# Two MLPs of a transformer kernel: the first product by pairs of output tiles with seven block products

## The chip, the cores and the metric

The kernel runs on one core of a Trainium2 chip. The metric is the time of the whole program on the device, in microseconds, as the median of three runs.

## The reference

The program computes two blocks of a transformer for 512 tokens of 1024 features, in float32. The change touches the squared-relu MLP, which the second block holds twice (`l` = 0 and 1), with 4096 hidden features:

```python
def squared_relu_mlp(h, w1, w2):
    return jnp.square(jax.nn.relu(h @ w1)) @ w2
...
        x = x + squared_relu_mlp(rms_norm_2(x, norm_mlp[layer]), mlp_w1[layer], mlp_w2[layer])
```

`h @ w1` is the first product, `... @ w2` the second. The attention and the mixers before, between and around the MLPs stay as they are.

## The kernel before

Activations stand feature-major: a tile holds 128 features as partitions and 512 tokens as columns. A float32 product is made of parts: each operand is split into a high part (a cast to float32r on ScalarE, `whi`, `xgh`, `hidh`) and a low part (the rest, a subtraction on VectorE, `wlo`, `xgl`, `hidl`), and `mm` (L287) multiplies high by high, high by low and low by high, three matmuls for each 128 rows of the contraction (L294 to L296). Each matmul is written with its own weight load.

`unit` (L254) loads one unit of weights, 128 x 1024 (the weights of one output tile for 8 tiles of the contraction, 512 KB), through SP's queue into a `raw` tile (L261), casts it (L269) and subtracts (L270). The pool `wp` holds two `raw`, two `whi` and two `wlo` tiles, used in turn. A tile is taken again when its last reader is done.

`mlp` (L901) goes through four chunks of 8 hidden tiles. In a chunk it makes the 8 hidden tiles one after the other (the first products: 8 x 3 matmuls of 512 columns into a PSUM bank of the ring `mm`, then relu out of PSUM (L917), square (L918) and the split into `hid` (L275, L276)), then 8 output tiles (the second products, from `hid`), each of which is scaled by R and added to x by VectorE (L909, L910). In the last chunk the last output tiles (4 in layer 0, 5 in layer 1) are made by halves of 256 tokens, so that what follows can begin with the first half.

PSUM has eight banks, cut into rings for a phase by `psum_phase`: in the MLPs six for `mm`, two for `t`.

The instructions are written in program order; a scheduler orders them for each engine when the program is built, by program order and by when it expects them to be ready, and sets the semaphores. On the chip each engine's order is then fixed. SP's queue issues the loads in order too, and a load whose buffer is not free holds those behind it.

## Time and profile before

| | us |
|---|---|
| median of three runs | 1986.74 |
| the three runs | 1985.92, 1986.74, 1994.5 |
| span of the profiled execution | 1986.7 |
| TensorE busy (share of the span) | 1906.8 (96%) |
| VectorE busy | 1169.8 (59%) |
| ScalarE busy | 885.8 (45%) |
| GpSimd busy | 400.8 (20%) |

The profiled execution's own time is its span; nothing lies around it. The profile tells for each engine when it was busy, with what, and what ended each idle time. PE stands for TensorE, PEld for its weight loads, DVE for VectorE, ACT for ScalarE, POOL for GpSimd, SP for the engine that issues the loads. A row of a matmul is longer than the distance to the next matmul's start, since matmuls overlap; the distance of the starts is the time that each takes of TensorE. PEclk is the granted clock of TensorE, as a share of its 2.4 GHz.

### The profile page before, as it was taken

The numbers are of one execution on the slowest core, as the hardware profiler recorded it, in microseconds if no ns is written. First come the engines' busy times: TensorE is split into PE (matmuls) and PEld (weight loads), VectorE is DVE, ScalarE is ACT, GpSimd is POOL, SyncE is SP. The second block draws the span as 40 slices with busy tenths as digits, with TensorE's granted clock in tenths as the row PEclk, the third lists the DMA queues.
The fourth block names the chain that finished last, engine by engine and source line by source line (L and its number), as shares of the span: only waits on it lengthen the run. The fifth ranks groups of instructions, "written<-read, shape, count | busy, mean of one in ns | idle before, by whom it ended". The sixth has DMA issues, their size and how long they took to land. (4 is left out here: it accounts for less than half of the span.)

```text
span 1986.7 us, 24617 instructions
## 1 busy us (share of the span) xinstructions
PE 1906.8 (96%) x9238; PEld 1566.1 (79%) x9238; DVE 1169.8 (59%) x1912; ACT 885.8 (45%) x1549; POOL 400.8 (20%) x374
## 2 busy tenths in 40 slices
PE   8688999999999999999999999989999999999997
PEld 6466788888888878888888888878878778888887
DVE  7979675335344874463434345869887963343435
ACT  6566654333233542234242434546666753324243
POOL 2777240000001420020000001235454430000001
PEclk9898999999999999999999999999999999999998
DMA  4121222222223222222223223254232122222222
GB/s 146 51 75 35 80 81 85 95 96 96 95 93 99 75 82 93 95 98 96 96 85 105 89 95 115 84 163 117 67 93 75 35 88 96 96 95 95 88 94 85
DMA packets 64551, 179.89 MB, mean 91 GB/s; under 512 B 7856, under 2 KB 16240, under 8 KB 64432
## 3 DMA queue, kind: packets, MB, share of 16 engines
q1 hardware_dynamic: 63600, 177.53, 28.0%
q8 instruction: 72, 1.18, 0.2%
q10 hardware_dynamic: 832, 0.79, 0.1%
q14 instruction: 47, 0.39, 0.1%
HBM read 165.71 MB, written 2.10 MB: 84 GB/s over the span
## 5 line engine op out<-in xcount | busy, mean ns | idle before, releaser
L269 ACT CAST whi<-raw 128x1024 fp32r<-128x1024 f32 (+4 forms) x324 | 303.6, 940 | 764.2 <-PE mm L295 680.6
L270 DVE TENSOR_TENSOR wlo<-raw,whi 128x1024 fp32r<-128x1024 f32 (+4 forms) x298 | 352.7, 1186 | 281.9 <-ACT whi L269 278.9
L294 PE MATMUL mm<-hidh,whi 128*128 128x512 f32 (+1 forms) x738 | 281.7, 382 | 1.0 <-DVE tmp L909 1.0
L296 PE MATMUL mm<-hidh,wlo 128*128 128x512 f32 (+1 forms) x738 | 281.4, 381 | 0.0
L295 PE MATMUL mm<-hidl,whi 128*128 128x512 f32 (+1 forms) x738 | 281.3, 381 | 0.0
L295 PE MATMUL mm<-xgl,whi 128*128 128x512 f32 (+1 forms) x608 | 233.6, 385 | 4.5 <-DVE xgl L279 3.2
L327 POOL TENSOR_TENSOR ssq<-ssq,sq 128x512 f32<-128x512 f32 (+1 forms) x61 | 71.8, 1177 | 810.2 <-ACT sq L324 809.1
L296 PE MATMUL mm<-xgh,wlo 128*128 128x512 f32 (+1 forms) x608 | 233.2, 384 | 0.4 <-DVE wlo L270 0.4
L294 PE MATMUL mm<-xgh,whi 128*128 128x512 f32 (+1 forms) x608 | 232.3, 385 | 0.6 <-ACT whi L269 0.6
L294 PEld LDWEIGHTS mm<-hidh,whi 128*128 128x128 f32 x738 | 138.4, 188 | 31.0 <-DVE tmp L909 1.2
L296 PEld LDWEIGHTS mm<-hidh,wlo 128*128 128x128 f32 x738 | 138.4, 188 | 29.8
L295 PEld LDWEIGHTS mm<-hidl,whi 128*128 128x128 f32 x738 | 138.4, 188 | 29.8
L295 PEld LDWEIGHTS mm<-xgl,whi 128*128 128x128 f32 x608 | 115.0, 189 | 31.0 <-DVE xgl L279 4.4
L909 DVE TENSOR_TENSOR tmp<-mm,R 128x512 f32<-128x512 f32 (+1 forms) x73 | 45.4, 624 | 155.6 <-PE mm L296 155.6
L294 PEld LDWEIGHTS mm<-xgh,whi 128*128 128x128 f32 x608 | 114.6, 189 | 25.8 <-ACT whi L269 1.5
L296 PEld LDWEIGHTS mm<-xgh,wlo 128*128 128x128 f32 x608 | 115.1, 189 | 24.7 <-DVE wlo L270 0.8
L411 ACT ACTIVATE pw<-pw,nm 128x512 f32<-128x512 f32 (+3 forms) x160 | 89.4, 560 | 55.5 <-DVE nm L409 54.5
L509 POOL TENSOR_TENSOR cy<-cy,tap 128x512 f32<-128x512 f32 x60 | 92.3, 1540 | 33.6 <-ACT tap L508 30.3
L276 DVE TENSOR_TENSOR hidl<-tmp,hidh 128x512 fp32r<-128x512 f32 x94 | 64.7, 689 | 37.0 <-ACT hidh L275 36.8
L511 DVE SCALAR_TENSOR_TENSOR cy<-cp,cols,cy 128x512 f32<-128x512 f32 x60 | 72.3, 1205 | 1.9 <-ACT cy L522 1.4
L409 DVE CUSTOM_DVE_ANT_0 pw<-s,tb 128x512 f32<-128x512 f32 (+3 forms) x128 | 59.0, 479 | 6.1 <-PE s L403 5.3
L276 DVE TENSOR_TENSOR ptl<-t,pth 128x384 fp32r<-128x384 f32 (+1 forms) x96 | 55.6, 591 | 9.1 <-ACT pth L275 9.0
(658 smaller groups left out, 4101.3 us busy)
## 6 DMA issues: line engine op xcount, KB each, us to landing
raw<-mlp SPq DMA_DIRECT2D x128, 512.0 KB, 3.4
raw<-a_in SPq DMA_DIRECT2D x24, 512.0 KB, 3.4
raw<-w_gate SPq DMA_DIRECT2D x22, 512.0 KB, 3.4
raw<-w_up SPq DMA_DIRECT2D x22, 512.0 KB, 3.4
raw<-w_down SPq DMA_DIRECT2D x16, 512.0 KB, 3.5
raw<-w_in SPq DMA_DIRECT2D x12, 512.0 KB, 3.6
raw<-a_out SPq DMA_DIRECT2D x8, 512.0 KB, 3.4
raw<-w_q SPq DMA_DIRECT2D x8, 512.0 KB, 3.8
```

Of the source, the lines that this page charges most:

```text
L269: S.copy(hi[:, a], raw[:, a])
L270: eng.tensor_tensor(lo[:, a], raw[:, a], hi[:, a], op=OP.subtract)
L276: (eng or V).tensor_tensor(l, src, h, op=OP.subtract)
L294: P.matmul(acc, hi[:, s], h, start=first and k == 0, stop=False)
L295: P.matmul(acc, hi[:, s], l, start=False, stop=False)
L296: P.matmul(acc, lo[:, s], h, start=False, stop=last and k == n - 1)
L327: (V if k >= self.n - 2 or self.fast else G).tensor_tensor(a, a, s[:, ts], op=OP.add)
L409: V.tensor_tensor_reduce(out=t, in0=s[:, :n], in1=tab[:, 384 - 128 * i:], op0=OP.add, op1=OP.min, scale=1.0, scalar=3.0e38, accum_out=nm[: ...
L411: S.activation(t, t, AF.Exp, bias=nm[:, i:i + 1], scale=-1.0, accum_out=rs[:, i:i + 1])
L509: G.tensor_tensor(conv_y[c], conv_y[c], t, op=OP.add)
L511: V.scalar_tensor_tensor(conv_y[c], cp[c][:, k:k + T], w, conv_y[c], op0=OP.mult, op1=OP.add)
L909: V.tensor_tensor(t, acc[:, ts], R[:, ts], op=OP.mult)
```

## The change

Two neighbouring output tiles of the first product, 2 x 2 blocks of weights (four contraction tiles each) and 2 x 2 blocks of inputs (the halves of the tokens, and the even and the odd contraction tiles) are multiplied with seven block products of sums in place of eight block products, in Winograd's form of Strassen's scheme. A block product is 4 x 3 matmuls of 256 columns. This is done for all pairs of a layer but the first, which stays two whole products: 15 pairs in each layer.

- The sums of the inputs (`pair_sums`) are made once per layer and kept split, four for each two contraction tiles.
- The sums of the weights are made in `pair_units`: of seven blocks of 128 x 512, which lie in a new order in DRAM (`_blocks`, 1792 KB for a pair), a tile `a` is loaded, a tile `s` is loaded and then another one added onto it by a DMA that GpSimd's queue issues, a half tile `z` is loaded, and a tile `u` is summed up on VectorE. Each of the four is split as before. Their `raw`, `whi` and `wlo` tiles come from `wp` and from a second pool of the same size, `sw`, in turn: a and u from `wp`, s and z from `sw`.
- `fast_pair` makes the products. The sums of products stay in PSUM where the scheme lets them: `y1` takes four of the products, `y4` two, `y2` one; three copies out of PSUM on ScalarE and three additions on VectorE make the two hidden tiles. The seventh product of a pair is written behind the fifth of the next (`late`).
- PSUM is cut into two banks `y1`, four `mm` and two `t`. In layer 1's last chunk four tiles instead of five go by halves. The weights of the halved tiles and the tiles of the output come from the two pools.

```diff
+def _blocks(w):
+    w = np.asarray(w)
+    m = w.shape[1]
+    a = w.reshape(4, 2, 128, m // 256, 2, 128).transpose(3, 4, 1, 2, 0, 5).reshape(m // 256, 2, 2, 128, 512)
+    b = [a[:, i, j] for i, j in ((0, 0), (0, 1), (1, 1), (0, 0), (1, 0), (1, 0), (1, 1))]
+    return np.ascontiguousarray(np.concatenate(b, 2))
...
-        A[f"mlp1_{l}"] = _units(I["mlp_w1_2"][l])
+        A[f"mlp1_{l}"] = _units(I["mlp_w1_2"][l])[:2]
+        A[f"mlp1f_{l}"] = _blocks(I["mlp_w1_2"][l])
...
+    B11, B12, B21, B22, T1, T3, T2, T4 = range(8)
+    def pair_sums(k, gain, pl, tpl):
+        b = pl.tile([128, 1024], FT, name="raw", bufs=2).rearrange("p (a t) -> p a t", a=4)
+        s = pl.tile([128, 1024], FT, name="raw", bufs=2).rearrange("p (a t) -> p a t", a=4)
+        for i in range(2):
+            S.activation(b[:, 2 * i:2 * i + 2], x[k + i].rearrange("p (a t) -> p a t", a=2), AF.Copy,
+                         scale=col(gain, k + i))
+        V.tensor_tensor(s[:, 0], b[:, B11], b[:, B12], op=OP.subtract)
+        V.tensor_tensor(s[:, 1], b[:, B22], b[:, B12], op=OP.subtract)
+        V.scalar_tensor_tensor(s[:, 2], s[:, 0], -1.0, b[:, B22], op0=OP.mult, op1=OP.subtract)
+        V.scalar_tensor_tensor(s[:, 3], s[:, 2], -1.0, b[:, B21], op0=OP.mult, op1=OP.subtract)
+        return split(s, *(tpl.tile([128, 4, T // 2], FR, name=f"xt{k}{p}") for p in "hl"))
+    def slots(tiles, sums):
+        return [[p[:, ts] for p in t] for t in tiles for ts in HALVES] + [[p[:, i] for p in sums] for i in range(4)]
+    def pair_units(src, rings):
+        def hl(r, n=1024):
+            pl = rings.pop(0)
+            rings.append(pl)
+            h, l = (pl.tile([128, 1024], FR, name=w, bufs=2)[:, :n] for w in ("whi", "wlo"))
+            return split(r[:, :n], h, l)
+        def raw():
+            pl = rings[0]
+            rings.append(rings.pop(0))
+            return pl.tile([128, 1024], FT, name="raw", bufs=2)
+        a, s, u, z = [raw() for _ in range(4)]
+        nc.sync.dma_start(a, src[:, :1024])
+        nc.sync.dma_start(s, src[:, 1024:2048])
+        nc.gpsimd.dma_start(s, src[:, 2048:3072], accum_op=OP.add)
+        nc.sync.dma_start(z[:, :512], src[:, 3072:])
+        ua = hl(a)
+        us = hl(s)
+        V.tensor_tensor(u[:, :512], s[:, 512:], z[:, :512], op=OP.add)
+        V.tensor_tensor(u[:, 512:], u[:, :512], a[:, 512:], op=OP.add)
+        return ua, us, hl(u), hl(z, 512)
+    late = []
+    def fast_pair(us, xps, pl, f, done):
+        ua, us_, uu, uz = us
+        H = T // 2
+        y1 = bank("y1")[:, :H]
+        y4 = bank("mm")[:, :H]
+        y2 = bank("mm")[:, :H]
+        def prod(acc, u, c0, slot, first):
+            hi, lo = u
+            for j, xp in enumerate(xps):
+                h, l = xp[slot]
+                s = slice(c0 + 128 * j, c0 + 128 * j + 128)
+                P.matmul(acc, hi[:, s], h, start=first and j == 0, stop=False, skip_group_check=True)
+                P.matmul(acc, hi[:, s], l, start=False, stop=False, skip_group_check=True)
+                P.matmul(acc, lo[:, s], h, start=False, stop=j == 3, skip_group_check=True)
+        def copy(acc):
+            t = pl.tile([128, H], FT, name="yc", bufs=4)
+            S.copy(t, acc)
+            return t
+        prod(y1, ua, 0, B11, True)
+        p1 = copy(y1)
+        prod(y4, us_, 0, T1, True)
+        p5 = copy(y4)
+        prod(y2, ua, 512, B21, True)
+        t1 = tmp()
+        V.tensor_tensor(t1[:, :H], y2, p1, op=OP.add)
+        prod(y1, uu, 0, T2, False)
+        u2 = copy(y1)
+        prod(y4, uu, 512, B22, False)
+        V.tensor_tensor(t1[:, H:], y4, u2, op=OP.add)
+        done(f, t1)
+        if late:
+            late.pop()()
+        prod(y1, us_, 512, T3, False)
+        t2 = tmp()
+        V.tensor_tensor(t2[:, H:], y1, p5, op=OP.add)
+        def last():
+            prod(y1, uz, 0, T4, False)
+            done(f + 1, t2, y1)
+        late.append(last)
...
+        sw = pool(f"sw{l}")
+        rings = [wp, sw]
+        tpl = pool(f"xt{l}")
+        xps = []
+        def hidden_tile(t, hid, f):
+            S.activation(t, t, AF.Square)
+            hid[f] = split_in(md, "hid", t, bufs=10)
         for ch in range(4):
-            hid = []
-            for f in range(8):
-                acc = ahead.pop(0) if ahead else gemm(A[f"mlp1_{l}"][8 * ch + f], xg)
-                t = tmp()
-                S.activation(t, acc, AF.Relu)
-                S.activation(t, t, AF.Square)
-                hid.append(split_in(md, "hid", t, bufs=10))
+            hid = [None] * 8
+            def done(f, t, acc=None, hid=hid):
+                if acc is None:
+                    S.activation(t, t, AF.Relu)
+                else:
+                    S.activation(t[:, T // 2:], t[:, T // 2:], AF.Relu, scale=-1.0)
+                    S.activation(t[:, :T // 2], acc, AF.Relu, scale=-1.0)
+                hidden_tile(t, hid, f)
+            for f in range(0, 8, 2):
+                if ch == 0 and f == 0:
+                    for i in range(2):
+                        acc = ahead.pop(0) if ahead else gemm(A[f"mlp1_{l}"][i], xg)
+                        t = tmp()
+                        S.activation(t, acc, AF.Relu)
+                        hidden_tile(t, hid, i)
+                    for k in range(0, KT, 2):
+                        xps.append(slots(xg[k:k + 2], pair_sums(k, f"norm_mlp{l}", sw, tpl)))
+                    continue
+                fast_pair(pair_units(A[f"mlp1f_{l}"][4 * ch + f // 2], rings), xps, md, f, done)
+            while late:
+                late.pop()()
...
-        us = {m: unit(A[f"mlp2_{l}_3"][m], dst=None if m > KT - 3 else
-                      [md.tile([128, 1024], FR, name=f"um{m}{p}") for p in "hl"]) for m in ms}
+        us = {m: unit(A[f"mlp2_{l}_3"][m], pl=[wp, sw][m % 2]) for m in ms}
...
+    psum_phase("ps2m", y1=2, mm=4, t=2)
+    mlp(0, md, xg, r5, 4, shared_norm, shared)
...
-    psum_phase("ps4", mm=6, t=2)
+    psum_phase("ps4", y1=2, mm=4, t=2)
...
-        t = md.tile([128, KT, T // 2], FT, name="out", bufs=2)
+        t = [pl.tile([128, 1024], FT, name="raw", bufs=2).rearrange("p (k t) -> p k t", k=4) for pl in pls]
...
-    mlp(1, md, xg, r6, 3, finish, ahead=ahead)
+    mlp(1, md, xg, r6, 4, finish, ahead=ahead)
```

## Rows read from the trace of the kernel before

**Rows 1.** Page part 1: busy time, share of the span, instructions of each engine

```profile
PE 1906.8 (96%) x9238; PEld 1566.1 (79%) x9238; DVE 1169.8 (59%) x1912; ACT 885.8 (45%) x1549; POOL 400.8 (20%) x374
```

**Rows 2.** Windows (us; busy us (count) per engine, clock, DMA share, GB/s): first, second products

```profile
900.00:942.00 42.00, 42.00 (x189) 34.25 (x188) 14.66 (x20) 20.09 (x29) 1.02 (x1) 1.00 0.30 100
942.00:987.00 45.00, 45.00 (x194) 36.15 (x193) 19.53 (x23) 10.16 (x11) 0.00 (x0) 1.00 0.28 93
```

**Rows 3.** Waits in 955 to 1225 (who, for whom: us, times, longest)

```profile
ACT whi L269 <- PE mm L295: 172.8, 47, 5.8
DVE wlo L270 <- ACT whi L269: 76.6, 27, 3.9
```

**Rows 4.** Timeline, TensorE, first products (start us, us, what): full width

```profile
1099.65 0.39 PE L294 MATMUL mm<-xg1h,whi 128*128 128x512 f32 x1
...
1111.96 0.40 PE L296 MATMUL mm<-xg2h,wlo 128*128 128x512 f32 x1
```

**Rows 5.** Timeline, TensorE: half width, in the MLP and elsewhere

```profile
1939.70 0.28 PE L294 MATMUL mm<-hidh,um3h 128*128 128x256 f32 x1
...
1941.85 0.28 PE L294 MATMUL mm<-hidh,um3h 128*128 128x256 f32 x1
...
1608.05 0.28 PE L295 MATMUL mm<-xg2l,whi 128*128 128x256 f32 x1
...
1610.28 0.28 PE L295 MATMUL t<-obl,whi 128*128 128x256 f32 x1
```

**Rows 6.** Groups by shape, ScalarE (busy us, mean ns, idle before): MLP and a PSUM copy

```profile
L269 ACT CAST whi<-raw 128x1024 fp32r<-128x1024 f32 x49 | 51.4, 1050 | 174.6 <-PE mm L295 172.8 <-DMA raw<-mlp 1.8
L918 ACT ACTIVATE tmp<-tmp 128x512 f32<-128x512 f32 x24 | 15.2, 633 | 0.8
L275 ACT CAST hidh<-tmp 128x512 fp32r<-128x512 f32 x24 | 14.9, 620 | 0.8
...
L269 ACT CAST whi<-raw 128x512 fp32r<-128x512 f32 x25 | 15.0, 616 | 8.0 <-PE mm L295 4.0 <-DMA raw<-phi_v 2.5 <-PE s L1064 1.2
...
L953 ACT COPY R<-t 128x256 f32<-128x256 f32 x1 | 0.4, 353 | 0.0
```

**Rows 7.** Groups by shape, VectorE: MLP

```profile
L270 DVE TENSOR_TENSOR wlo<-raw,whi 128x1024 fp32r<-128x1024 f32 x49 | 59.8, 1221 | 76.6 <-ACT whi L269 76.6
L910 DVE TENSOR_TENSOR x<-x,tmp 128x512 f32<-128x512 f32 x26 | 17.9, 690 | 0.7
L276 DVE TENSOR_TENSOR hidl<-tmp,hidh 128x512 fp32r<-128x512 f32 x24 | 16.6, 692 | 14.1 <-ACT hidh L275 14.1
...
L909 DVE TENSOR_TENSOR tmp<-mm,R 128x256 f32<-128x256 f32 x18 | 7.5, 419 | 8.8 <-PE mm L296 8.8
```

**Rows 8.** DMA issues (count, KB each, median us from issue to landing)

```profile
raw<-mlp SPq DMA_DIRECT2D x128, 512.0 KB, 3.4
...
raw<-w_v SPq DMA_DIRECT2D x4, 512.0 KB, 4.4
...
raw<-b_o SPq DMA_DIRECT2D x16, 128.0 KB, 2.0
```

**Rows 9.** Tile raw: the issuing instruction on SP, ns min/median/max

```profile
L261 SPq DMA_DIRECT2D raw<-mlp x128: 327/328/328, 882.5 to 1945.3; - x128
```

**Rows 10.** Windows: inputs of layer 1's MLP

```profile
1604.00:1620.40 16.40, 16.22 (x104) 15.02 (x105) 15.89 (x34) 13.18 (x33) 7.57 (x10) 0.88 0.10 36
```

**Rows 11.** Timeline, TensorE: last matmul of layer 1's second whole product

```profile
1631.04 0.39 PE L296 MATMUL mm<-xg7h,wlo 128*128 128x512 f32 x1
```

**Rows 12.** Windows: granted clock behind an idle stretch

```profile
1600.00:1602.00 2.00, 0.35 (x1) 0.19 (x1) 2.00 (x2) 0.00 (x0) 1.91 (x1) 0.77 0.85 258
1602.00:1608.00 6.00, 5.48 (x24) 5.19 (x25) 5.36 (x13) 3.25 (x9) 2.24 (x3) 0.51 0.30 89
1608.00:1612.00 4.00, 3.94 (x33) 3.74 (x33) 4.00 (x10) 3.40 (x10) 1.58 (x3) 1.00 0.00 0
```

More of the change, by code (lines that the diff above doesn't have):

```diff
@@ L899, in _body, with mlp @@
         sx.add(x[m])
-    def mlp(l, md, xg, r, full, done, ready=None, ahead=()):
+    def mlp(l, md, xg, r, full, finished, ready=None, ahead=()):
         R = row_tile(r, square=True)
@@ L936, in mlp @@
                 sx.add(x[m], ts)
-            done(sx.rstd(ts=ts), ts)
+            finished(sx.rstd(ts=ts), ts, rings)
+        tpl.release()
+        sw.release()
     xgp.release()
@@ L950, in shared, with shared_norm @@
         split(x[m][:, ts], *(p[:, ts] for p in xs[m]))
-    def shared_norm(c, ts):
+    def shared_norm(c, ts, pls):
         S.copy(R5[:, ts], rows(c, None, ts)[:, ts])
-    mlp(0, md, xg, sx.rstd(), 4, shared_norm, shared)
+    r5 = sx.rstd()
+    psum_phase("ps2m", y1=2, mm=4, t=2)
+    mlp(0, md, xg, r5, 4, shared_norm, shared)
     md.release()
@@ L1252, in _body, with finish @@
     md = pool("md5", right=True)
-    def finish(c, ts):
-        t = md.tile([128, KT, T // 2], FT, name="out", bufs=2)
+    def finish(c, ts, pls):
+        t = [pl.tile([128, 1024], FT, name="raw", bufs=2).rearrange("p (k t) -> p k t", k=4) for pl in pls]
         for k in range(KT):
-            S.activation(t[:, k], x[k][:, ts], AF.Copy, scale=col("final_norm", k))
+            S.activation(t[k // 4][:, k % 4], x[k][:, ts], AF.Copy, scale=col("final_norm", k))
         RF = rows(c, None, ts)[:, ts]
-        k0 = 0
         for k in range(KT):
-            V.tensor_tensor(t[:, k], t[:, k], RF, op=OP.mult)
+            tk = t[k // 4]
+            V.tensor_tensor(tk[:, k % 4], tk[:, k % 4], RF, op=OP.mult)
             if k in (3, 5, 7):
+                k0 = {3: 0, 5: 4, 7: 6}[k]
                 (nc.scalar if k == 5 else nc.sync).dma_start(
-                    out.rearrange("k p t -> p k t")[:, k0:k + 1, ts], t[:, k0:k + 1])
-                k0 = k + 1
-    mlp(1, md, xg, r6, 3, finish, ahead=ahead)
+                    out.rearrange("k p t -> p k t")[:, k0:k + 1, ts], tk[:, k0 % 4:k % 4 + 1])
+    mlp(1, md, xg, r6, 4, finish, ahead=ahead)
     md.release()
```

## Prediction

> **What bounds the kernel now.** I read the busy shares first: TensorE is busy for 96% of the span [rows 1]. An average over stages does not say what a stage waits for, so next come the stretches of the MLP of layer 0. In its first products and in its second products TensorE has no idle time at 2.4 GHz (granted clock 1.00), while VectorE is busy for 35% and 43%, ScalarE for 48% and 23%, GpSimd hardly, the DMA engines for 30% and 28% [rows 2]. The waits agree: what ScalarE's weight cast waits for is TensorE (172.8 us in 47 waits), so weights are loaded long before they are wanted and only wait for a buffer [rows 3]. So TensorE's matmuls set the time here, and a matmul saved is time saved until another engine or the loads become late.
>
> The busy time of a matmul row (0.39 us) overlaps the next one, so the price is the distance between starts: 53 distances in 12.31 us for 512 columns, 0.2323 us each [rows 4]; 18 in 2.15 us, 0.1194 us, for 256 columns behind the MLP's tiles, and 19 in 2.23 us, 0.1174 us, elsewhere [rows 5]. A half-width matmul, each with its own weight load, costs 0.505 to 0.514 of a full one, so the smaller blocks are almost free of extra cost per instruction.
>
> **The matmuls.** A pair of output tiles takes 2 x 8 x 3 = 48 matmuls of 512 columns now, 48 x 0.2323 = 11.15 us. The seven block products take 7 x 4 x 3 = 84 of 256 columns, 84 x 0.1194 = 10.03 us (9.86 at the other row). Each layer has 16 pairs, and its first stays as it was: 30 pairs in all. Saved: 30 x 1.12 = 33.6 us (38.7 at the other row). I take 0.1194, since those rows are from this stage.
>
> **The work beside them.** Per pair ScalarE gets three casts of 1024 columns (1.05 each), one of 512 (0.62), three copies of 256 columns out of PSUM (0.35 each), a relu of 512 (0.63) and two of 256 (about 0.38 each), two squares (0.63), two casts of the hidden tiles (0.62): 8.7 us [rows 6]. VectorE gets three subtractions of 1024 (1.22), one of 512 (0.69), two sums of weights of 512 (0.69), three additions of 256 (0.42) and two subtractions of hidden tiles (0.69): 8.4 us [rows 7]. Both fit into 10.03 us and so cost nothing while TensorE covers them, but at 87% and 84% there is little cover: the order on each is fixed, and a cast that waits for a load holds the copies that TensorE needs next.
>
> **The weights' way** is the disputed part. Before, a unit's way was load, cast, subtraction, with two buffers of each. Now a pair takes four raw tiles, which are all four that the two pools have. One of them, s, is loaded (512 KB), then a second DMA from GpSimd's queue adds 512 KB onto it; it must wait for the first. Then come two sums on VectorE, the casts and subtractions, and only then is the buffer free for the next pair's s. SP's queue holds the pair's other loads (a, s, z) in that order, so whatever waits for a buffer at its head holds the next; the mlp2 units are queued behind a chunk's last pair.
>
> The plain load takes 3.4 us from issue to landing [rows 8]. The trace has no accumulating DMA, so I bound it: not below 3.4, the same bytes written plainly; not above 7.8, two such loads one behind the other plus 1.0 for GpSimd's issue. (SP's issue is 0.33 us [rows 9], GpSimd's unknown.) Between them: 128 KB land in 2.0 us and 512 KB in 3.4 [rows 8], so about 1.5 us of the 3.4 grow with the bytes and 1.9 do not. An addition reads the target too; with the growing part doubled and an issue like SP's that is 1.9 + 3.0 + 0.3 = 5.2. I take 5.1, near the plain load's row.
>
> The Trainium skill (page "DMA: Bandwidth & Descriptors", section "Anatomy of one DMA — SWDGE (gpsimd) path") fits a DMA from GpSimd as 2.0 us + bytes / 436 GB/s, an estimate of 3.2 us for 512 KB; no run here shows it, and by it the additions would cause no stall at all (1958, below). Its page "Collectives: The Full Stack", section "The bandwidth ceiling: the fold count and why AG ≠ RS ≠ AR", speaks against this change: it says an add in the DMA engines runs at half a copy's rate because it reads two sources; by that and the same fit an estimate is 4.4 us, and the sum below would be 1961.
>
> Now a chunk of four pairs, time 0 at its first matmul, a product 1.43 us. Pair 1 was loaded under the second products before. Pair 2's s is added up early, but its split must wait until pair 1's sixth product (8.6 us) has read the tiles: 8.6 + 1.05 + 1.22, and an estimated 0.2 for hand-overs, make 11.1. It is wanted from 10.3 on: 0.8 late. Pair 3's s can be loaded from 11.1: landed 14.6, added 19.8, split with one VectorE sum ahead 22.5; pair 3 begins at 19.4 and wants it at 21.1: 1.3 late. Pair 4's s, from 22.5: split at 33.9; wanted at 32.4: 1.4 late. Products that need s neither directly nor by a sum (the third, the seventh of the pair before) fill up to 2.9 us if they stand earlier in TensorE's order than the source has them. So 0 to 3.5 us a chunk of four, 0 to 2.1 in the chunk of three, 0 to 25 us for two layers. I take half, 13. Beyond 5.1 each further us of the addition delays pair 3 by one and pair 4 by one more: 2 x (3 x 2 + 1) = 14 us for both layers.
>
> **The start of each layer.** The block sums of the inputs are, four times per layer, two scalings (0.63), four sums of 256 (0.42), a cast and a subtraction of 1024: 9.2 us of ScalarE, 11.6 of VectorE. In layer 0 most of x is final long before, and two whole products lie ahead (11 us): 1 us. In layer 1 the inputs come late: VectorE is busy for 15.89 of 16.40 us until 1620.4 [rows 10]; then come 11.6 us of sums and some 6 us of splits of weights and hidden tiles, so to 1638, while TensorE ends the second whole product at 1631.3 [rows 11] and has two products (2.9 us) that need no sum. 4 us late. Together 5, from 0 to 12.
>
> **The rest.** PSUM is cut to four banks for whole products instead of six. VectorE frees such a bank about 1.4 us after a product (two operations of 0.69 [rows 7]), so one spare bank of 5.58 us covers it: 0. In the last chunk of layer 1 four tiles instead of five go by halves, and four weight units come from the pools: the second halves, 4 x 2.9 us, still cover the first halves' finish; 0, or 2 us if the cover is short. Bytes per pair go from 1024 KB to 1792 KB. At 93 GB/s the DMA engines were busy for 0.28 [rows 2]; at 183 GB/s that is 0.55, and 0.16 more if the addition's extra read counts. The rate holds; a load behind another lands later (4.4 us for w_v [rows 8]), which is in the upper bound.
>
> **The sum.** The profiled execution's span is 1986.7 us, the median of the runs 1986.74, nothing lies between. 1986.7 - 33.6 + 13 + 5 = 1971.1.
>
> **Rivals.** (1) *The addition is slow and the weights set the pace.* The terms cancel where 33.6 = 5 + 13 + 14 x (D - 5.1): at D = 6.2 us from issue to landing. At 7.8 the stalls are 51 us: 1986.7 - 33.6 + 5 + 51 = 2009. Waits of some us also cost clock: after TensorE stood still for most of 1600 to 1602 its granted clock was 0.51 for the next 6 us, the 1.2 GHz level, and 1.00 later [rows 12]. A few such falls add 3 us each, 2020. For it: four tiles, a chain of two DMAs, a cast and a subtraction in each cycle. Against it: 45 us of second products in each chunk in which only two units' loads are in flight. (2) *No stall*: the addition lands as the plain load does, or TensorE's order takes the ready products first: 1986.7 - 33.6 + 5 = 1958. For it: all DMA engines idle for 70% and GpSimd idle [rows 2]. (3) *ScalarE's and VectorE's fixed orders give it back*: with both at 85%, a pair need only lose 1.0 us (a cast of 1.05 us ahead of a copy of 0.35 that TensorE waits for) and 30 us are gone: about 1987. (4) That the change does not remove the matmuls it says: the counts above come from the diff's loops; no chance given.
>
> **Chances.** Forecast (1960 to 1977) 0.32; no stall (1948 to 1960) 0.21; given back (1977 to 1997) 0.20; slow addition 0.27. A measurement of this kernel can tell about 0.5%, 10 us, from no change. Faster by more: 0.53; within: 0.20; slower by more: 0.27. The range takes in the forecast, given back, most of no stall and of the slow addition: 1954 to 2012. The likeliest case's own range is 1960 to 1977.
>
> **What the profile will show.** Matmuls of 256 columns in the first products at 0.117 to 0.120 us; some 84 per pair; stretches of four pairs at 40 us and second products at 44.6. TensorE's idle time should stand before the product with s (the second of a pair), released by the cast or subtraction of whi or wlo, and grow from pair 2 to pair 4; ScalarE's cast should wait for a DMA, no longer for TensorE. The addition's time from issue to landing decides between the cases. A clock under 1.00 in the first products, idle time of over 2 us per pair, or waits for the copies out of PSUM would prove the forecast wrong.

## The result, and the profile after

The changed kernel takes 2066.76 us (median of 4 runs, 2066.07 to 2068.32), the kernel before beside it 1989.88 (1985.92 to 1994.5): a ratio of 1.0388, 95% interval 1.0369 to 1.0408. The profiled execution's span went from 1986.7 to 2064.8 us, 78.1 more. The forecast was 1971, its range ended at 2012, and the dearest case of its rivals at 2020.

Page of the changed kernel, part 1 (busy us, share of the span, instructions) and the new queue of part 3 (packets, MB, share of 16 engines' time):

```profile
PE 1908.5 (92%) x10294; PEld 1608.8 (78%) x10294; DVE 1314.8 (64%) x2160; ACT 977.4 (47%) x1752; POOL 428.8 (21%) x403
...
q0 software_dynamic: 4320, 15.73, 4.7%
```

Beside [rows 1]: TensorE is as long busy as before (1908.5 against 1906.8 us) although it has less to multiply, and busy for 92% instead of 96% of the span. It stands still more, and behind some standstills its matmuls run slower (shown below at 1135 and at 1677 us). What it waits for, in the view of waits (who, for whom: us in all, times, longest):

```profile
PE mm L380 <- ACT whi L286: 34.0, 13, 14.8
PE y L382 <- DVE wlo L287: 14.0, 13, 5.3
...
PE y L380 <- ACT whi L286: 5.5, 4, 3.8
PE t L447 <- DVE ssq L432: 4.9, 3, 3.4
```

and what ScalarE's casts of the pairs' weights wait for:

```profile
ACT whi L286 <- DMA raw<-mlp1f: 81.0, 29, 9.6
```

In [rows 3] the cast waited for TensorE: weights were there early. Now it waits for a DMA in 29 places: weights come late.

### The profile page after: what moved, and what is told of

Same layout as the page of the kernel before. It is cut to its first block, busy times and chain, and to the rows that moved or that the text cites. A ratio compares the mean times of both kernels' runs of the same rounds, so it can differ in the third digit from the quotient of the medians.

```text
span 2064.8 us, 27438 instructions
## 1 busy us (share of the span) xinstructions
PE 1908.5 (92%) x10294; PEld 1608.8 (78%) x10294; DVE 1314.8 (64%) x2160; ACT 977.4 (47%) x1752; POOL 428.8 (21%) x403
## 4 chain that ended last, share of the span: by engine, by line
PE 65%; DVE 16%; DMA 9%; ACT 5%; issue 4%; POOL 1%; DVEq 0%; SPq 0%; POOLq 0%; ACTq 0%
PE mm L305 17%; PE mm L307 17%; PE mm L306 16%; DMA raw<-mlp1f 7%; DVE cy L616 2%; DVE wlo L281 2%; PE s L508 2%; PE y L382 1%; PE o L541 1%; PE y L380 1%; PE y L381 1%; PE t L533 1%; PE mm L380 1%; DVE wlo L287 1%; PE mm L382 1%
## 5 line engine op out<-in xcount | busy, mean ns | idle before, releaser
L280 ACT CAST whi<-raw 128x1024 fp32r<-128x1024 f32 (+4 forms) x269 | 245.8, 919 | 533.9 <-PE mm L306 427.4
L281 DVE TENSOR_TENSOR wlo<-raw,whi 128x1024 fp32r<-128x1024 f32 (+3 forms) x243 | 288.0, 1188 | 109.2 <-ACT whi L280 106.2
L305 PE MATMUL mm<-hidh,whi 128*128 128x512 f32 (+1 forms) x810 | 302.8, 377 | 6.9 <-ACT whi L280 5.6
L307 PE MATMUL mm<-hidh,wlo 128*128 128x512 f32 (+1 forms) x810 | 301.8, 375 | 4.7 <-DVE wlo L281 4.7
L306 PE MATMUL mm<-hidl,whi 128*128 128x512 f32 (+1 forms) x810 | 303.3, 375 | 1.4 <-DVE hidl L287 1.4
L286 ACT CAST whi<-raw 128x1024 fp32r<-128x1024 f32 (+1 forms) x120 | 111.3, 942 | 178.8 <-DMA raw<-mlp1f 81.0
L307 PEld LDWEIGHTS mm<-hidh,wlo 128*128 128x128 f32 x810 | 151.9, 188 | 37.0 <-DVE wlo L281 8.9
L306 PEld LDWEIGHTS mm<-hidl,whi 128*128 128x128 f32 x810 | 152.0, 188 | 32.9 <-DVE hidl L287 4.8
L287 DVE TENSOR_TENSOR wlo<-raw,whi 128x1024 fp32r<-128x1024 f32 (+1 forms) x120 | 129.6, 1088 | 50.9 <-ACT whi L286 36.7
L356 POOL DMA_DIRECT2D raw<-mlp1f x30 | 26.3, 876 | 620.4 <-DMA raw<-mlp1f 296.8
```

The lines of the kernel that those rows point to most:

```text
L280: S.copy(hi[:, a], raw[:, a])
L281: eng.tensor_tensor(lo[:, a], raw[:, a], hi[:, a], op=OP.subtract)
L286: S.copy(h, src)
L287: (eng or V).tensor_tensor(l, src, h, op=OP.subtract)
L305: P.matmul(acc, hi[:, s], h, start=first and k == 0, stop=False)
L306: P.matmul(acc, hi[:, s], l, start=False, stop=False)
```

## Where the time came from

The timeline of TensorE gives the start of each stage's first matmul. A "stretch" is a quarter of a layer, its first products and the second products behind them, counted together, because TensorE's order puts one unit of second products (24 matmuls, 5.6 us) among the pairs' products. (The expectations speak of the first products without that unit.)

| stage (us) | before | after | difference |
|---|---|---|---|
| projection of the convolution's stage, ahead of layer 0 | 44.79 | 49.24 | +4.45 |
| layer 0, first stretch | 90.76 | 103.23 | +12.47 |
| layer 0, three later stretches | 270.97 | 283.79 | +12.82 |
| attention between | 347.19 | 348.71 | +1.52 |
| layer 1, first stretch | 98.64 | 130.09 | +31.45 |
| layer 1, three later stretches | 270.62 | 285.22 | +14.60 |
| head and tail | | | +0.79 |

The sum is 78.1. So the two first stretches, with six of the 30 pairs, became longer by more than the six later ones together (43.9 against 27.4 us).

The matmuls themselves became as cheap as forecast: from 1004.11 to 1007.30 us there are 27 distances of 256 columns, 0.1181 us each. A pair is then 84 x 0.1181 = 9.92 us for 11.15, and 30 pairs save 36.9. The stalls are therefore 78.1 + 36.9 = 115 us: 16.2 in layer 0's first stretch, 35.1 in layer 1's, 56.9 in the six later ones, 4.5 at the cut, 2.3 elsewhere.

**A later stretch.** One stretch of layer 0 in windows (us; busy us (count) of each engine, clock, DMA share, GB/s), first and second products, of the kernel before and of the changed one:

```profile
987.24:1031.86 44.62, 44.62 (x194) 36.18 (x192) 15.93 (x17) 20.65 (x30) 0.00 (x0) 1.00 0.29 95
1031.86:1076.65 44.79, 44.79 (x194) 35.98 (x192) 19.54 (x23) 10.17 (x12) 0.00 (x0) 1.00 0.28 94
```

```profile
1004.11:1058.72 54.61, 49.44 (x364) 45.56 (x362) 31.68 (x43) 31.11 (x53) 2.60 (x3) 1.00 0.56 142
1058.72:1099.11 40.39, 39.21 (x168) 30.32 (x167) 20.13 (x25) 9.42 (x11) 0.87 (x1) 1.00 0.34 95
```

VectorE is busy for 58% and ScalarE for 57% of the first products' window, DMA for 56%: no engine is full. It is a chain that sets the pace. In the next stretch one tile's cycle is seen whole; timeline (start us, us, what, [idle before <- releaser]) of SP, GpSimd, ScalarE, VectorE and TensorE for the tile s of two pairs, some rows of it, put in order of time:

```profile
1109.60 0.33 SPq L355 DMA_DIRECT2D raw<-mlp1f  x1
1113.69 0.88 POOL L356 DMA_DIRECT2D raw<-mlp1f  x1 [17.88 <-DMA raw<-mlp1f]
1120.66 1.04 ACT L286 CAST whi<-raw 128x1024 fp32r<-128x1024 f32 x1 [2.99 <-DMA raw<-mlp1f]
1121.75 0.39 PE L380 MATMUL mm<-xt0h,whi 128*128 128x256 f32 x1 [1.67 <-ACT whi L286]
1121.98 0.28 PE L381 MATMUL mm<-xt0l,whi 128*128 128x256 f32 x1
1122.10 0.28 PE L380 MATMUL mm<-xg1h,whi 128*128 128x256 f32 x1
1122.51 1.22 DVE L287 TENSOR_TENSOR wlo<-raw,whi 128x1024 fp32r<-128x1024 f32 x1
1123.76 0.33 SPq L355 DMA_DIRECT2D raw<-mlp1f  x1
1128.89 0.88 POOL L356 DMA_DIRECT2D raw<-mlp1f  x1 [14.32 <-DVE wlo L287]
1134.64 1.04 ACT L286 CAST whi<-raw 128x1024 fp32r<-128x1024 f32 x1 [2.90 <-DMA raw<-mlp1f]
1135.74 0.39 PE L380 MATMUL mm<-xt0h,whi 128*128 128x256 f32 x1 [1.81 <-ACT whi L286]
```

The tile is loaded, added to, cast, subtracted from, and only then loaded anew: 14.2 us from load to load, 14.0 from cast to cast, where TensorE has 9.9 us of products. Of the 14.2, 4.1 go by until the addition is issued, 7.0 until the cast, and 3.1 until VectorE, which makes two sums of weights first, has subtracted and the tile is free. The idle times in the rows (1.67, 1.81) are less than what is lost. From the matmul ahead of the wait (1119.81) to the one behind it 1.94 us pass, 1.82 more than usual, and the next starts 0.23 us later instead of 0.118: the wait of 1.67 us cost 1.93. Behind the second of these waits the granted clock fell: in the 5 us from 1135 on it is 0.72, a mean of its two levels, 2.4 and 1.2 GHz (TensorE alone: busy (count), clock, DMA share, GB/s):

```profile
1135.00:1140.00 5.00, 4.26 (x25) 0.72 0.52 175
```

**Layer 1's first stretch.** The last of the inputs' block sums on VectorE, the cast of it, and behind it the first pair that wants sums:

```profile
1666.15 0.42 DVE L333 SCALAR_TENSOR_TENSOR raw<-raw 128x256 f32<-128x256 f32 x1
1666.61 1.04 ACT L286 CAST xt6h<-raw 128x1024 fp32r<-128x1024 f32 x1 [1.05 <-DVE raw L333]
1666.66 0.33 SPq L355 DMA_DIRECT2D raw<-mlp1f  x1
1670.68 0.93 POOL L356 DMA_DIRECT2D raw<-mlp1f  x1 [9.85 <-DMA raw<-mlp1f]
1676.69 2.52 ACT L286 CAST whi<-raw 128x1024 fp32r<-128x1024 f32 x3 [9.04 <-DMA raw<-mlp1f]
1677.79 0.58 PE L380 MATMUL mm<-xt0h,whi 128*128 128x256 f32 x1 [14.78 <-ACT whi L286]
```

The load of s is issued 0.09 us after the last block sum has read its raw tile: `pair_sums` takes its two tiles from the same ring `raw` of the layer's pool that s and z come from. Sums and loads, which could lie side by side, follow one another: TensorE stands for 14.78 us. Behind it the clock is low again (17.80 us at 0.68, 22.20 at 0.80; window, all engines):

```profile
1660.00:1677.80 17.80, 2.02 (x17) 1.65 (x15) 8.32 (x16) 7.71 (x14) 1.75 (x2) 0.68 0.35 74
1677.80:1700.00 22.20, 17.65 (x112) 17.24 (x113) 10.85 (x15) 8.49 (x13) 1.10 (x2) 0.80 0.48 131
```

**Ahead of layer 0** TensorE stands once, before the matmuls of the sum of squares:

```profile
900.00 1.02 PE L447 MATMUL t<-ones,ssq 128*128 128x1 f32 x8 [3.40 <-DVE ssq L432]
```

Before, the whole products of the layer ran ahead of these matmuls. With the new cut of PSUM they cannot, since the new banks come free only when the old phase's last user, this sum, is done.

## The experiments

The theories. W: the cycle of s's raw tile (load, addition, cast, subtraction) sets the pace of the later pairs. O, its rival: the fixed orders of ScalarE and VectorE do, whatever the loads do. L: the layers' starts lose their time to the block sums of the inputs. P: the cut of PSUM holds the first whole products. (S and R come up with e12 and e13.) All results in one table; "middle" is the mean of the second and third stretches of both layers, "span" that of the profiled execution. Ahead of the MLPs, where all these kernels but e4 are alike in the source, the spans alone differ by up to 5 us (the projection starts at 847.9 to 853.0 us), so stretches tell more than spans, above all where a kernel ran once.

| kernel (us) | layer 0, first | layer 1, first | middle | span |
|---|---|---|---|---|
| before | 90.76 | 98.64 | 89.50 | 1986.7 |
| after | 103.23 | 130.09 | 94.66 | 2064.8 |
| e1 s not added to | 91.84 | 114.84 | 87.76 | 1991.5 |
| e2 third raw tile | 91.86 | 117.49 | 89.29 | 2013.9 |
| e3 no block sums of inputs | 95.63 | 107.20 | 94.39 | 2033.4 |
| e4 early cut | 105.39 | 130.48 | 94.80 | 2071.7 |
| e5 other order | 102.26 | 128.67 | 98.24 | 2080.3 |
| e6 no cut | 104.41 | 130.32 | 94.51 | 2062.5 |
| e7 whole first stretches | 94.42 | 103.32 | 94.42 | 2030.2 |
| e9 s overwritten | 98.10 | 124.26 | 90.87 | 2027.7 |
| e10 mends, order of the change | 91.48 | 103.02 | 88.39 | 1985.9 |
| e11 mends and other order | 91.27 | 104.25 | 86.53 | 1977.3 |
| e12 as e11, one pool | 95.01 | 104.39 | 88.89 | 1991.5 |
| e13 sums in a tile of their own | 96.22 | 121.26 | 94.38 | 2052.7 |
| e14 as e11, half whole | 92.19 | 105.48 | 86.35 | 1979.5 |

### e1: s is loaded, nothing is added to it

```
-        nc.gpsimd.dma_start(s, src[:, 2048:3072], accum_op=OP.add)
```

> The accumulating DMA is left out: s is loaded once and stays one block of the weights instead of the sum of two. Theory W (the weights' way: s's tile comes free, is loaded in 3.7 us, added to in 6.5, cast and subtracted, 14 us in all against 10.0 us of products) expects the six later stretches of first products to fall from 45.5 to 48.7 us to 40 to 43, and the whole from 2064.8 us to 2020 to 2035. Theory O (the fixed orders of ScalarE and VectorE, whatever the loads do) expects them to stay at 45 or more, and the whole above 2055. Both expect the first stretch of each layer to lose some us too, 3 to 10, since three pairs lie in it.

1993.33 us, 73 less than the changed kernel: more than W expected. The middle stretches fell by 6.9 us, and the first stretches by 11.4 and 15.3. All of ScalarE's and VectorE's work on the pairs is still there, but not all of it in the same order: with the addition gone the scheduler set some casts and sums anew. The windows of a stretch:

```profile
990.54:1036.90 46.36, 46.08 (x358) 44.52 (x357) 31.58 (x43) 30.41 (x53) 0.00 (x0) 1.00 0.39 120
1036.90:1078.08 41.18, 40.00 (x173) 31.41 (x172) 20.11 (x25) 9.40 (x11) 0.00 (x0) 1.00 0.33 96
```

In the first products 0.28 us of TensorE are idle. So the amount of work on the two engines is not the limit: 31.58 and 30.41 us of it in 46.36 delay nothing once s is early. That fits W. It does not rule O out, since a part of the order changed with the edit; e9 leaves the order as it is. What is left stands at the start of the second products:

```profile
1042.41 0.50 PE L305 MATMUL mm<-hidh,whi 128*128 128x512 f32 x1 [0.45 <-ACT whi L280]
...
1043.36 0.50 PE L305 MATMUL mm<-hidh,whi 128*128 128x512 f32 x1 [0.22 <-ACT whi L280]
...
1044.61 0.50 PE L307 MATMUL mm<-hidh,wlo 128*128 128x512 f32 x1 [0.52 <-DVE wlo L281]
```

### e2: a third raw tile in the layer's pool

```
-            return pl.tile([128, 1024], FT, name="raw", bufs=2)
+            return pl.tile([128, 1024], FT, name="raw", bufs=nb[id(pl)])    # 2 in wp, 3 in the layer's pool
```

> The pool of the layer gets a third raw tile, so that the next pair's s can be loaded and added to while the present one is still being split; all is computed as in the changed kernel. Theory W expects the addition's 6.5 us to go under the products: stretches of 40 to 43 us, the whole at 2020 to 2040. If instead the addition's own duration sets the pace wherever it stands, or the engines' orders do (theory O), the stretches stay above 45 and the whole above 2055.

2015.66 us, 51 less and a little more than W expected, with the additions in place (they now take 6.1 us to land). The middle stretches fell by 5.4 of the 6.9 us that e1 won. So it is not the addition's length as such, it is that one tile has to go round in it: with a second tile for s it lies mostly under the products. Here too the scheduler set the order anew, and what that is worth was not measured apart.

### e3: the inputs are not summed

```
-                        xps.append(slots(xg[k:k + 2], pair_sums(k, f"norm_mlp{l}", sw, tpl)))
+                        xps.append(slots(xg[k:k + 2], ()) + slots(xg[k:k + 2], ()))
```

> The block sums of the inputs are left out: products that want a sum read a part of x instead. Theory L (the sums on VectorE and ScalarE hold the first stretch of each layer) expects the first stretch of layer 0 to fall from 55.1 us to 45 to 49 and that of layer 1 from 82 to 55 to 60, the whole to 2064.8 - 30 = 2030 to 2040, and TensorE's idle 14.8 us before the product with s in layer 1 to be gone. The rival (these stretches lose their time to the loads, as the others do) expects under 10 us from the whole.

2035.17 us, as L expected. Layer 1's first stretch became 22.9 us shorter, layer 0's 7.6 (the stage ahead took 3.3 us of these back), the middle ones stayed (94.39). In layer 1 TensorE's longest wait there is now 2.8 us. Whether it is the sums' time or their tiles is left to e13.

### e4: PSUM is cut earlier

```
-    psum_phase("ps2", mm=6, t=2)
+    psum_phase("ps2", y1=2, mm=4, t=2)
...
-    psum_phase("ps2m", y1=2, mm=4, t=2)
```

> PSUM is cut into 2, 4 and 2 banks already ahead of the convolution's stage, so there is no cut ahead of layer 0. Theory P (the cut makes the first whole product wait for the old cut's last user, the sum of squares) expects TensorE's 3.4 us of idle time ahead of layer 0 to go and the stage before it to last 44.8 us again, the whole 4 to 5 us less, 2060. If four banks are too few in the stages ahead, they lose what this wins, and the whole is 2064 or more.

2073.55 us, 7 more. The projection ahead of layer 0 takes 44.80 us again, so P's wait is gone. But the stages ahead of it, which now have four banks for whole products instead of six, end 10.5 us later (862.09 for 851.64): in them up to five products of the source hold a bank each at once, which may be why. Four banks are dear where six were used.

### e5: another order of a pair's products

```
         prod(y1, ua, 0, B11, True)
         p1 = copy(y1)
-        prod(y4, us_, 0, T1, True)
-        p5 = copy(y4)
         prod(y2, ua, 512, B21, True)
...
+        if late:
+            late.pop()()
+        prod(y4, us_, 0, T1, True)
+        p5 = copy(y4)
...
-        if late:
-            late.pop()()
```

> The seven products of a pair stand in another order in the source: those with a first (first and third), then the seventh of the pair before, then those with s and the sums, so that TensorE has 4.3 us of products between the last use of a pair's s and the first use of the next one, instead of 1.4. Theory W (the raw tile's cycle of load, addition and cast takes 14 us and sets the pace) expects little, 0 to 10 us off the whole, since the cycle is not touched. The rival (the split of s that waits for its two parts' tiles is what TensorE stands for) expects two thirds of the later stretches' loss back, 2045 or less.

2082.12 us, 15 more: neither theory had that. The middle stretches are 3.6 us longer. The timeline shows why; VectorE, TensorE and ScalarE around one pair:

```profile
1123.43 0.69 DVE L360 TENSOR_TENSOR raw<-raw 128x512 f32<-128x512 f32 x1 [7.66 <-DMA raw<-mlp1f]
1124.15 0.69 DVE L361 TENSOR_TENSOR raw<-raw 128x512 f32<-128x512 f32 x1
1124.76 0.42 DVE L401 TENSOR_TENSOR tmp<-mm,yc 128x256 f32<-128x256 f32 x1
1125.10 0.41 DVE L405 TENSOR_TENSOR tmp<-y,yc 128x256 f32<-128x256 f32 x1
...
1125.57 0.58 PE L380 MATMUL y<-xt0h,whi 128*128 128x256 f32 x1 [4.24 <-DVE tmp L405]
...
1124.93 1.04 ACT L286 CAST whi<-raw 128x1024 fp32r<-128x1024 f32 x1 [7.25 <-DVE raw L361]
```

VectorE's sum of weights waits 7.66 us for the DMA into s. Behind it in VectorE's order stand the additions of the pair before, and the last of them (L405) must have read its bank before the seventh product may write to it. The seventh product, which needs nothing of s, now stands ahead of those with s, and waits 4.24 us for s all the same, through VectorE. So O is not wrong altogether: where s is early nothing waits for the other engines (e1), but one late DMA at the head of VectorE's and ScalarE's queues is passed on to work that does not need it.

### e6: no new cut

```
-    psum_phase("ps2m", y1=2, mm=4, t=2)
...
-    psum_phase("ps4", y1=2, mm=4, t=2)
+    psum_phase("ps4", mm=6, t=2)
...
-        y1 = bank("y1")[:, :H]
+        y1 = bank("t")[:, :H]
```

> PSUM stays cut as before the change, six banks and two, with no new cut ahead of layer 0: the products that had a ring of their own use the two banks that serve the sums of squares. Theory P (the cut alone holds TensorE ahead of layer 0) expects 4 to 6 us off the whole, 2059 to 2061, TensorE's 3.4 us of idle time before the sum of squares gone, and nothing lost in the stages ahead, since they keep their six banks. The rival (two whole products had to wait for a bank anyway, as the sums on VectorE are late) expects 2063 or more.

2064.27 us, 2.5 less than the changed kernel's median: the whole is what the rival expected, not P. The wait is gone and the stage ahead takes 44.80 us, 4.4 less, and 1.4 of that came back in the first stretches of the two layers (104.41 and 130.32), where the weights are late anyway. A single run doesn't tell 2 us; that the wait belongs to the cut is shown by the stage, not by the whole.

### e7: whole products in the first stretches

```
-                if ch == 0 and f == 0:
+                if ch == 0 and f < WHOLE[l]:          # (8, 8)
...
-                    for k in range(0, KT, 2):
+                    for k in range(0, KT if f == SUMS[l] else 0, 2):    # (6, 6)
```

> All four pairs of each layer's first stretch are done as whole products, as before the change, and the block sums of the inputs are issued behind them; the saving of six pairs, 6.7 us, is given up. Theory L with W (sums and loads cost the two first stretches some 42 us) expects these stretches at 45 to 47 us again, and 35 us off the whole, about 2028. The rival (the sums only move on, and stand in the way of the second products or the next stretch) expects under 15 us.

2031.99 us, 35 less, as expected within 4 us, although the saving of six pairs is given up: 8.8 us in layer 0's first stretch and 26.8 in layer 1's. Issued behind four pairs of whole products, sums and loads lie under them.

### e9: the second block overwrites the first

```
-        nc.gpsimd.dma_start(s, src[:, 2048:3072], accum_op=OP.add)
+        nc.gpsimd.dma_start(s, src[:, 2048:3072])
```

> GpSimd's DMA into s writes plainly over the loaded block instead of adding to it, with the same bytes, the same queue and the same place in the chain; s is then one block instead of a sum of two. It measures what of the 6.5 us from issue to landing (an SP load of as many bytes: 3.7) is the addition's. If the addition is the cost (the target is read too), the overwriting lands in 4 to 5 us, the six later stretches fall by 1.5 to 2.5 us a pair, to 47 to 50, and the whole to 2035 to 2045. If GpSimd's queue is the cost, whatever it carries, it lands in 6 us or more and the whole stays above 2055.

2029.57 us, 37 less than the changed kernel and more than expected. DMA issues (KB each, median us from issue to landing) and the queue, of the changed kernel and of this one:

```profile
raw<-mlp1f SPq DMA_DIRECT2D x60, 512.0 KB, 3.7
raw<-mlp1f POOLq DMA_DIRECT2D x30, 512.0 KB, 6.5
```

```profile
q0 software_dynamic: 4320, 15.73, 2.5%
...
raw<-mlp1f POOLq DMA_DIRECT2D x30, 512.0 KB, 4.0
```

From GpSimd's queue a plain 512 KB lands in 4.0 us, from SP's in 3.7: the queue is not the cost. With the addition it is 6.5, and the packets take 4.7% of 2064.8 us instead of 2.5% of 2027.7, 1.9 times as long. The 2.5 us are worth 3.8 us of each middle stretch, 5.1 and 5.8 of the first ones. This is the cleanest of the experiments. In the traces of this kernel and of the changed one every engine carries out the same instructions in the same order (10294 on TensorE, 2160 on VectorE, 1752 on ScalarE), so no order explains the gain, and O alone, whatever the loads do, falls. From the projection to the end the kernel takes 33.4 us less; the other 3.7 lie ahead of it, where the two kernels are alike.

### e8, e10, e11, e12, e14: the mends together

e8 and e11 are one kernel: e2's tile, e5's order, e6's banks, e7's whole products, and the weights of the second products from both pools in turn:

```
-                add(m, gemm(A[f"mlp2_{l}_{ch}"][m], hid))
+                add(m, gemm(None, hid, unit(A[f"mlp2_{l}_{ch}"][m], pl=[wp, sw][m % 2], bufs=(2 + m % 2, 2))))
```

> Third raw tile, other order of the products, PSUM as before the change, whole products in the first stretches, and weights of the second products from both pools in turn, all together. If the losses stand apart as the budget has it (later stretches 40, second products 16 to 21, layer starts 42, cut 4.5), their removal at the price of 6.7 us of saving gives 2064.8 - 40 - 18 - 42 - 4.5 + 6.7 = 1967, below the kernel before. If they share a cause, or the engines' orders hold part of them (theory O), it stays at 1985 or above.

> The kernel with all the mends and the other order again, timed in three rounds against the kernel before. One look gave 1972 us beside 1990. If that holds it is 0.988 to 0.994 of the kernel before.

The first run took 1972.08 us beside 1989.66; four more take 1977.52 us (1973.43 to 1979.97), 0.9944 of the kernel before, interval 0.9925 to 0.9964: 4% less than the changed kernel, and a gain over the kernel before that is clear of noise but small, 0.6%. One of its stretches:

```profile
989.36:1030.93 41.57, 41.32 (x330) 40.15 (x329) 25.34 (x37) 27.46 (x48) 1.73 (x2) 1.00 0.62 165
1030.93:1075.68 44.75, 44.40 (x203) 36.01 (x202) 25.92 (x34) 12.87 (x17) 1.73 (x2) 1.00 0.41 106
```

The middle stretches are at 86.53 us, 3.0 less than before; four pairs save at most 4.9.

e10 has the order of the change instead (e5's edit taken back):

> All the mends together (third raw tile, PSUM as before the change, whole products in the first stretches, weights of the second products from both pools), but the seven products in the order that the change has. The other order alone cost 15 us, which theory W explains by the casts' order on ScalarE while the raw tile's cycle sets the pace; with a third raw tile that cycle is gone. W expects the two orders within 8 us of each other, the new order ahead by 0 to 8 since it leaves 4.3 us instead of 1.4 for the split of s: 1970 to 1980. The rival (the new order is worse by itself, each pair by 0.5 us) expects 1958 to 1965.

1995.21 us (1987.87 to 2001.72), ratio 1.0035 (1.0016 to 1.0054): the other order is 0.9% better here by the medians, 17.7 us, twice what W allowed it, where it was worse without the third tile. No run of e10 is as fast as the slowest of e11, but the size is loose: the two profiled executions are 8.6 us apart. Their middle stretches differ by 1.9 us. The wait is now the one that was worked out before the result for a pair's second product (the split of s, which needs the tiles that the sixth product of the pair before has just read), and the products in front of it cover it; e10, then e11:

```profile
1020.79 0.38 PE L382 MATMUL mm<-xt0h,whi 128*128 128x256 f32 x1 [2.26 <-ACT whi L286]
```

```profile
1011.19 0.38 PE L382 MATMUL mm<-xt0h,whi 128*128 128x256 f32 x1 [0.25 <-ACT whi L286]
```

e12 takes all weights of second products from one pool, as the change does:

> All the mends and the other order, but the weights of the second products come from one pool, as in the change. Theory S (in the second products' starts TensorE waits for casts that stand in ScalarE's order behind one that waits for a tile) expects TensorE's idle 1.2 us at the start of each stretch of second products back and 2 us each lost with what lies around it, 8 x 2 = 16 us, 1985 to 1990. The rival (those waits came from the same cycle of s and are gone with it) expects 1970 to 1975.

1993.5 us, 16 more than e11, 3.5 above what S expected. The middle stretches lose 2.4 us. In ScalarE's order the cast of the next pair's z stands ahead of the casts of these weights, and waits for the last product to release its tile:

```profile
1039.34 0.62 ACT L286 CAST whi<-raw 128x512 fp32r<-128x512 f32 x1 [3.89 <-PE t L383]
...
1042.87 2.00 ACT L280 CAST whi<-raw 128x1024 fp32r<-128x1024 f32 x2 [1.32 <-PE mm L306]
```

TensorE waits 0.45 us at 1043.97 and again behind it. With four tiles instead of two the weights are cast before that.

e14 does two pairs of each first stretch whole instead of four:

> All the mends and the other order, but only four of eight products of each first stretch are whole ones, the block sums behind the second. Four more pairs than in e11_all_timed are done with seven products, 4.5 us of saving. If four whole products (22 us) cover the sums, the loads and the additions, it is 2 to 5 us faster than e11_all_timed, 1973 to 1976 beside its 1977.5. If layer 1's sums are still late behind 22 us, TensorE stands in layer 1's first stretch, and it is 0 to 8 us slower.

1980.66 us (1979.22 to 1983.88), 0.9948 of the kernel before (0.9928 to 0.9969). That can't be told from e11: the four more pairs with seven products win nothing, since both first stretches became about 1 us longer (92.19 and 105.48).

### e13: the block sums in a tile of their own

```
-        s = pl.tile([128, 1024], FT, name="raw", bufs=2).rearrange("p (a t) -> p a t", a=4)
...
+        b = pl.tile([128, 1024], FT, name="sums", bufs=1).rearrange("p (a t) -> p a t", a=4)
+        V.tensor_tensor(b[:, 0], b[:, B11], b[:, B12], op=OP.subtract)
```

> The changed kernel, but the block sums of the inputs are formed in place in one tile of their own, so that the raw tiles are free for the first pair's loads at once. Theory R (in layer 1 the 14.8 us of TensorE's idle time are the load and the addition of s, which start only when the sums give its tile back) expects that idle time at 2 to 7 us, layer 1's first stretch 9 to 14 us shorter, layer 0's 0 to 4, and the whole at 2048 to 2056. The rival (the sums' own time on VectorE and ScalarE) expects the same stretch or a longer one, since one tile in place of two makes the four sums follow one another, and 2062 to 2072.

2054.45 us, 12 less, as R expected of the whole. The load of s is issued at 1623.91 us and its addition at 1630.53, under the attention's end, and the wait of 14.78 us has become three shorter ones:

```profile
1667.29 1.12 PE L472 MATMUL t<-ident,r 128*128 128x128 f32 x4 [5.41 <-DVE r L462]
1669.35 0.58 PE L381 MATMUL y<-xg0h,wlo 128*128 128x256 f32 x1 [0.51 <-DVE wlo L287]
1675.96 0.58 PE L379 MATMUL mm<-xt6h,whi 128*128 128x256 f32 x1 [2.66 <-ACT xt6h L286]
```

Layer 1's first stretch is 8.8 us shorter, layer 0's 7.0 (the stage ahead took 3.2 of these back). So of the 22.9 us that e3 won in layer 1 some 9 are the tiles that the sums take from the weights. That the rest, 14, is the sums' own work ahead of what TensorE needs is likely, not shown: the last wait above is for a sum, but with one tile the sums also follow one another here, which may cost part of what the edit wins.

## Why the prediction was wrong

**Right.** The 256 columns (0.1181 us for the 0.1194 taken), and with them a saving of 36.9 us for 33.6. TensorE's idle time does stand before the product with s, released by the cast, and the cast does wait for a DMA. The rival that decided is the first one, the slow addition, with its break-even at 6.2 us: the addition took 6.5. By the prediction's own slope it would have given 1971 + 14 x 1.4 = 1991, and it gave 2065, so four more steps failed. The slope itself held: the 2.5 us between e9's landing and the changed kernel's cost 33.4 us from the projection on, where 14 for each us makes 35. That is partly luck, since a middle stretch moved by 3.8 us for the 5 of the slope, and the first ones by 5.1 and 5.8 for 2.5. What the slope starts from was wrong: at 4.0 us the sum has no stall left, 1958, and e9 took 2029.57.

**The addition, 5.1 us.** It took 6.5. Doubling the growing part gave 5.2; the addition adds 2.5 us to a plain DMA on the same queue (4.0, e9), 1.7 times that growing part of 1.5. From the fit on the page "DMA: Bandwidth & Descriptors" of the Trainium skill, section "Anatomy of one DMA — SWDGE (gpsimd) path", an estimate for a plain one is 3.2 us; here that is 4.0. The page "Collectives: The Full Stack" of the Trainium skill, in its section "The bandwidth ceiling: the fold count and why AG ≠ RS ≠ AR", puts the adding phase of a collective at half the rate of the copying one, because the add reads two sources. The packets' time here agrees (1.9 times); the estimate of 4.4 us made from it does not (6.5).

**The weights' stalls, 13 us.** The six later stretches lost 56.9. Three things were mis-sized. The first is the cycle of s: worked out at 11.4 us from split to split (3.5 for the load, 5.2 for the addition, 2.7 for the split), it is 14.2 in the rows above (4.1, 7.0 and 3.1), so the load and the split were too short as well. The second is that half of the stalls was written off because products that need no s would fill in. In the changed kernel the third product stands behind the first two matmuls with s (1122.10 us) and can't fill the wait for the cast; e5 puts it and the seventh ahead, and the seventh waits all the same, because VectorE's sum waits for s at the head of its queue, and what the seventh needs is behind it. The third is that a wait was counted at its length; the one in the rows above cost 0.26 us more, and the clock fell behind the next. Without the addition, and with the order that the scheduler then set, e1 wins 6.9 us a stretch, 41 for six. The rest, some 15, is the next step.

**The second products, 0 us.** They were taken to be unaffected, as their weights were early before. But they share ScalarE's order with the pairs' casts, and a cast that waits for a tile stands ahead of them: 2.4 us a stretch, 16 us in all (e12 against e11, with the other mends in place).

**The start of each layer, 5 us.** The largest error: with their share of the saving the first stretches lost 16.2 and 35.1 us. The sum went over the time of the block sums on VectorE, and left out which tiles they are formed in. They hold the ring that s is loaded into, so load, addition and sums are added up instead of lying side by side (e13: 8.8 us in layer 1, 3.8 in layer 0). The addition's chain costs 15.3 and 11.4 us here (e1), the sums with their tiles 22.9 and 4.3 (e3); these overlap and can't be added.

**The cut of PSUM, 0 us.** The working asked whether four banks are enough behind the cut. It did not ask what the cut itself waits for: 4.45 us ahead of layer 0. e6 shows that the wait goes with the cut, though hardly what that is worth in the whole as long as the weights are late behind it.

**What stays open.** Of the 4.9 us that a middle stretch of e11 could win it wins 3.0; the missing 1.9 were not traced further. How much of what e1 and e2 won is the new order was not separated. Nor was the clock's part of the 115 us: the mean granted clock of the span fell from 0.981 to 0.970, from which an estimate is at most 0.030 x 2064.8 - 0.019 x 1986.7 = 24 us, since TensorE was not busy all the time that the clock was low.

## What to carry to other kernels

Before a loop is given a longer chain per tile, work out each tile's round trip (free, load, add, cast, split, last reader) and hold it against the work of one turn; a second tile for the one that goes round longest was worth 51 us here (with the order that came with it), more than the whole saving aimed at. Look up for every new temporary which ring it is taken from and what else waits for that ring, and for every waiting instruction what stands behind it on its engine: a late DMA at the head of an in-order queue reaches work that never touches the data. A saving in the engine that bounds the kernel needs the others' work to be ready when it starts; where it is not (the start of a layer), the old form is the faster one.

## What the runs showed of the hardware

An accumulating DMA of 512 KB from GpSimd's queue took 6.5 us from issue to landing in the changed kernel (5.7 to 7.0 in the others), the same DMA without the addition 4.0, a load from SP's queue 3.7; its packets kept the DMA engines busy 1.9 times as long. Issuing it kept GpSimd for 0.87 us, the plain one for 0.54.

A matmul of 256 columns behind 256 columns costs 0.118 us, but a wait of 1.67 us ahead of one cost 1.93 us, since the matmuls around it start further apart too; the wait of 1.81 us cost 2.07. So short waits cost more than their idle time here. After TensorE stood still for 14.8 us the granted clock of the next 22 us was 0.80, a mean of its two levels, 2.4 and 1.2 GHz.
